# Score products of a gated recurrence on four groups of partitions, and two gate products moved between the last two heads

## The chip, the core and the metric

The kernel runs on one core of a Trainium2 chip. The metric is the time on the device of one execution, in microseconds (us). The core has a matrix engine (TensorE, PE in the profile; its loads of the stationary operand are listed apart as PEld), a vector engine (VectorE, DVE), a scalar engine (ScalarE, ACT), a general engine (GpSimd, POOL) and an engine that starts transfers (SyncE, SP). Each works through its own list in order, and they wait for each other by semaphores.

## The reference

Two layers on 1024 tokens of width 1024. Layer 0 is windowed attention; the change does not touch it. Layer 1 is a gated linear recurrence (HGRN2) with 8 heads of key and value width 128:

```python
proj = h @ w_in                       # q, f, i, z
q = silu(q)
log_f = logaddexp(log(lb), log1p(-lb) + log_sigmoid(f))
k = -expm1(log_f);  v = i
# per head, over time:  S = S * exp(log_f) + k v^T ;  o = q S
# in chunks: scores[t, s] = sum_k q[t] k[s] exp(b[t] - b[s])  for s <= t,  b = cumsum(log_f)
o = o * rsqrt(mean(o * o) + eps) * gnorm_w
y = (o * silu(z)) @ w_out
```

Each layer is wrapped in two norms and added to its input.

## The kernel before

All large projections are done in three products: both operands are split into a high and a low part, and `product` (L189) adds high x high, high x low and low x high. A projection of 128 x 512 is one unit of 24 such products, into one of two buffers of PSUM (tag "mm").

`mixer1` is layer 1. Its `plan` is a list of units in the order in which they are written: `i_unit` (values), `qf_unit` (q, and f with k, of one head in halves of 512 tokens), `rec(h)` (the recurrence of a head), `z_unit(c, t)` (the gate: a projection, a sigmoid on ScalarE at L868, a product on VectorE at L869, and one on GpSimd that multiplies it into the values, L870). The order of the plan gives priorities; the order on each engine is worked out by a scheduler from them, so that units of the plan interleave on the engines. What `rec(h)` needs on VectorE and GpSimd is done while TensorE works on the projections of the next unit.

`rec(h)` calls `scores_block` on the usual path (the other, `scores_tree`, is not run with these inputs). The tokens are in 8 blocks of 128, and keys stand in the stationary operand, queries in the moving one; the key width of 128 is summed over:

- Two scans on VectorE (L757, L758) give the running products U and V of the gate in sub-blocks of 16. Q and K are multiplied by them (L759, L760), and the totals of sub-blocks go to a small tile `tt` (L769 to L774). U and V are then reused for the scaled operands of the lowest level (L776 to L779); Q and K are scaled for the levels above (L780, L781), and from there are called X and Y.
- L788 computes all scores within blocks of 32 (32 products of 32 keys by 32 queries, tile `psd`). Output partition is key, and the 32 keys of a product lie at partitions 0, 32, 64 or 96: four groups in turns. L792 copies the causal part to the score tile `sc`.
- L797 computes the scores between the two blocks of 32 in a block of 64: 16 products of 32 by 32, into partitions 0 to 31 and 64 to 95 of `pss`. L801 copies them to `sc`.
- X and Y are scaled once more (L806 VectorE, L807 GpSimd), and L812 computes the scores between the two blocks of 64 in a block of 128: 8 products of 64 keys by 64 queries, all into partitions 0 to 63. L814 copies them.
- A last scaling gives the operands between blocks of 128. `rec` then transposes Y (L828), forms key-value products (L834), runs the state through the 8 blocks on VectorE (L838, L840), and adds scores x values (L847) and X x state (L849). Each half is normed (L852, L215, L217, L855).

The tiles `psd`, `pss` share two buffers of PSUM (tag "s"). Weights come in order through SP's queue, are split by ScalarE (L154) and VectorE (L155), and a weight's place is free for the next after its last product.

Of the kernel before, what the change touches and what calls it, by code (L numbers as in the profile page):

```python
# [12 lines left out]
F32 = mybir.dt.float32  # L13
# [4 lines left out]
AF = mybir.ActivationFunctionType  # L18
# [5 lines left out]
P = 128  # L24
# [65 lines left out]
def emit(tc, I, out):  # L90
    nc = tc.nc
# [3 lines left out]
    with top:  # L95
# [4 lines left out]
        pp = top.enter_context(tc.tile_pool(name="ps", bufs=2, space=PSUM))  # L100
# [565 lines left out]
        def mixer1(fast, vo, rp):  # L666
# [11 lines left out]
            def qf_unit(h, isf, half):  # L678
                ps = proj_feat(60 + 4 * h + 2 * isf + 8 * (h // 4), half)
                cs = slice(half * 512, (half + 1) * 512)  # L680
                if (h, isf) not in qfk:
                    if isf and fast:
                        qfk[h, 1] = Fs[h % 2]
                    else:
                        qfk[h, isf] = rp.tile([P, T], F32, tag="qf"[isf], bufs=2 if isf else nb3, name="qf")
                dst = qfk[h, isf][:, cs]
                if not isf:
                    sg = rp.tile([P, 512], F32, tag="sg", bufs=2, name="sg")
                    nc.scalar.activation(sg, ps, AF.Sigmoid)
                    v.tensor_tensor(dst, ps, sg, op=ALU.mult)  # L690
                else:
                    if (h, 2) not in qfk:
                        qfk[h, 2] = rp.tile([P, T], F32, tag="k", bufs=nb3, name="kk")
                    kk = qfk[h, 2][:, cs]
                    lb, ol = lbt[:, 1, h:h + 1], lbt[:, 0, h:h + 1]
                    nc.scalar.activation(dst, ps, AF.Sigmoid)  # L696
                    nc.scalar.activation(kk, ps, AF.Sigmoid, scale=-1.0)
                    nc.gpsimd.tensor_scalar(dst, dst, ol, lb, op0=ALU.mult, op1=ALU.add)  # L698
                    nc.gpsimd.tensor_scalar(kk, kk, ol, 1.0, op0=ALU.mult, op1=ALU.mult)
# [48 lines left out]
            def scores_block(h, Q, F, K):  # L748


                sc = scs[h % 2]

                v.tensor_copy(F1[:, ::16], F[:, :T:16])
                nc.gpsimd.memset(F[:, :T:16], 0.0)
                U = rp.tile([P, T], F32, tag="U", name="U")
                V = rp.tile([P, T], F32, tag="V", name="V")
                v.tensor_tensor_scan(U, F[:, :T], F1, 0.0, op0=ALU.mult, op1=ALU.add)  # L757
                v.tensor_tensor_scan(V[:, ::-1], F[:, T:0:-1], E1[:, ::-1], 0.0, op0=ALU.mult, op1=ALU.add)  # L758
                v.tensor_tensor(Q, Q, U, op=ALU.mult)  # L759
                v.tensor_tensor(K, K, V, op=ALU.mult)  # L760

                def blk(a, n):
                    return a.rearrange("p (b two n) -> p b two n", two=2, n=n)

                tt = rp.tile([P, 6, 32], F32, tag="tt", bufs=2, name="tt")
                t32, t64, t128 = tt[:, 4, :], tt[:, 5, :16], tt[:, 5, 16:24]
                e1, e2, r1, r2 = (tt[:, i, :].unsqueeze(2).to_broadcast([P, 32, 16]) for i in range(4))
                for i in range(2):
                    v.tensor_copy(tt[:, i, :], U[:, 16 * i + 15::32])  # L769
                v.reciprocal(tt[:, 2:4, :], tt[:, 0:2, :])  # L770
                v.tensor_tensor(t32, tt[:, 0, :], tt[:, 1, :], op=ALU.mult)
                for a, b in ((t64, t32), (t128, t64)):
                    bv = b.rearrange("p (b two) -> p b two", two=2)
                    v.tensor_tensor(a, bv[:, :, 0], bv[:, :, 1], op=ALU.mult)  # L774
                Q2, K2, M2, N2 = blk(Q, 16), blk(K, 16), blk(U, 16), blk(V, 16)
                v.tensor_tensor(M2[:, :, 0, :], Q2[:, :, 0, :], r1, op=ALU.mult)  # L776
                nc.gpsimd.tensor_copy(M2[:, :, 1, :], Q2[:, :, 1, :])
                nc.gpsimd.tensor_copy(N2[:, :, 0, :], K2[:, :, 0, :])
                v.tensor_tensor(N2[:, :, 1, :], K2[:, :, 1, :], r2, op=ALU.mult)  # L779
                v.tensor_tensor(Q2[:, :, 1, :], Q2[:, :, 1, :], e1, op=ALU.mult)  # L780
                nc.gpsimd.tensor_tensor(K2[:, :, 0, :], K2[:, :, 0, :], e2, op=ALU.mult)  # L781
                X, Y = Q, K

                ps = pp.tile([P, 8, 32], F32, tag="s", name="psd")
                for c in range(8):
                    for o in range(0, P, 32):
                        cs = slice(c * P + o, c * P + o + 32)
                        nc.tensor.matmul(ps[o:o + 32, c, :], V[:, cs], U[:, cs], start=True, stop=True)  # L788
                for o in range(0, P, 32):
                    r = slice(o, o + 32)  # L790
                    mk = msk[r, M_D - M_L + o:M_D - M_L + o + 32]
                    v.copy_predicated(sc[r, :, r], mk.unsqueeze(1).to_broadcast([32, 8, 32]), ps[r])  # L792
                ps = pp.tile([P, 8, 64], F32, tag="s", name="pss")
                for c in range(8):
                    for j in range(2):
                        o = c * P + 64 * j
                        nc.tensor.matmul(ps[64 * j:64 * j + 32, c, :32], Y[:, o:o + 32], X[:, o + 32:o + 64],  # L797
                                         start=True, stop=True)
                for j in range(2):
                    o = 64 * j  # L800
                    nc.scalar.activation(sc[o:o + 32, :, o + 32:o + 64], ps[o:o + 32, :, :32], AF.Copy)  # L801
                for n, tot in ((32, t32), (64, t64)):
                    Xv, Yv = blk(X, n), blk(Y, n)
                    nb = T // (2 * n)
                    tv = tot.rearrange("p (b two) -> p b two", two=2)
                    v.tensor_tensor(Xv[:, :, 1, :], Xv[:, :, 1, :], tv[:, :, 0:1].to_broadcast([P, nb, n]), op=ALU.mult)  # L806
                    nc.gpsimd.tensor_tensor(Yv[:, :, 0, :], Yv[:, :, 0, :], tv[:, :, 1:2].to_broadcast([P, nb, n]),  # L807
                                            op=ALU.mult)
                    if n == 32:
                        ps = pp.tile([P, 8, 64], F32, tag="s", name="pss")  # L810
                        for c in range(8):
                            nc.tensor.matmul(ps[:64, c, :], Y[:, c * P:c * P + 64], X[:, c * P + 64:(c + 1) * P],  # L812
                                             start=True, stop=True)
                        nc.scalar.activation(sc[:64, :, 64:], ps[:64], AF.Copy)  # L814
                return sc, X, Y, t128

            def rec(h):
                vt = vo[h // 4]
                hc = slice((h % 4) * P, (h % 4 + 1) * P)
                ins = (qfk[h, 0], qfk[h, 1], qfk[h, 2])  # L820
                sc, X, Y, tot = scores_block(h, *ins) if fast else scores_tree(*ins)
                yn = rp.tile([P, 8, P], F32, tag="yn", name="yn")
                S = rp.tile([P, 8, P], F32, tag="S", name="S")
# [41 lines left out]
            def z_unit(c, t):  # L865
                ps = proj_nat(100 + 8 * c, t)
                sg = rp.tile([P, 512], F32, tag="sg", bufs=2, name="sg")
                nc.scalar.activation(sg, ps, AF.Sigmoid)  # L868
                v.tensor_tensor(sg, ps, sg, op=ALU.mult)  # L869
                nc.gpsimd.tensor_tensor(vo[c][:, t, :], vo[c][:, t, :], sg, op=ALU.mult)  # L870

            QF = [(0, 0), (1, 0), (0, 1), (1, 1)]
            qf = lambda h: [lambda u=u: qf_unit(h, *u) for u in QF]
            iu = lambda c: [lambda t=t: i_unit(c, t) for t in range(8)]
            zu = lambda c: [lambda t=t: z_unit(c, t) for t in range(8)]
            rc = lambda h: [lambda: rec(h)]
            plan = iu(0) + qf(0) + ([zeros] if fast else []) + qf(1) + rc(0) + qf(2) + rc(1) + qf(3) + rc(2) + iu(1) + rc(3)
            plan += qf(4) + qf(5) + rc(4) + qf(6) + rc(5) + qf(7) + rc(6) + rc(7) + zu(0)
            for u in plan:
                u()  # L880
            for t in range(5):
# [163 lines left out]
```

## Time and profile before

| | |
|---|---|
| median of 3 runs | 920.67 us (918.2, 920.67, 920.74) |
| profiled execution | 919.34 us, span 917.5 us |
| granted TensorE clock | 0.995 of full, mean |
| TensorE busy | 891.1 us, 97% |
| VectorE / ScalarE / GpSimd busy | 551.2 / 373.7 / 342.1 us |
| the stage of the heads | about 480 to 745 us of the span |

The span runs from the first instruction to the last; what is left of the time lies around it. In the rows of the profile, a line such as L812 is a line of the kernel before; `out<-in` are the program's tile names; `128*32 128x32` is the shape of the array used and that of the operand. PE rows give matrix products, PEld rows loads of the stationary operand. A row of the timeline merges successive instructions of one line. In brackets stands the idle time ahead of the row and who ended it. The row of a stage gives start and end, its length, then busy time and count for PE, PEld, DVE, ACT and POOL, the granted clock, the share of the DMA engines and GB/s.

### The profile page before, as it was taken

How to read it: one execution, taken by the hardware profiler on the slowest of the kernel's cores; microseconds unless marked ns; L12 is line 12 of the kernel's file. 1: busy time of each engine (PE TensorE's matmuls, PEld its weight loads, DVE VectorE, ACT ScalarE, POOL GpSimd, SP SyncE). 2: the span in 40 equal slices, each digit the busy share in tenths (PEclk: the TensorE clock that was granted, in tenths of full speed). 3: DMA queues.
4: the chain of work that ended last, by engine and by line, in shares of the span. 5: the costliest groups of instructions: out<-in, count | busy, mean ns of one | idle time of the engine just before them, and what ended most of it. 6: DMA issues, size and time to landing. Idle time of an engine off the chain costs nothing.

```text
span 917.5 us, 14082 instructions
## 1 busy us (share of the span) xinstructions
PE 891.1 (97%) x5214; PEld 744.8 (81%) x5214; DVE 551.2 (60%) x911; ACT 373.7 (41%) x958; POOL 342.1 (37%) x506
## 2 busy tenths in 40 slices
PE   6989999999999999999999999999999999999996
PEld 4868888888887788878888888888888788888885
DVE  6858887777876535762278864246866924252243
ACT  6525667666656332542322331423334124242311
POOL 5504465667787202330054422115424433210011
PEclk9999999999999999999999999999999999999998
DMA  8455364512311223540311010121111003032053
GB/s 285 143 153 157 107 185 130 166 54 62 90 54 59 91 63 129 177 149 19 106 50 36 24 47 1 51 66 35 35 47 48 1 1 92 1 98 86 24 183 119
DMA packets 53255, 78.61 MB, mean 86 GB/s; under 512 B 4760, under 2 KB 24984, under 8 KB 53176
## 3 DMA queue, kind: packets, MB, share of 16 engines
q1 hardware_dynamic: 53032, 77.51, 27.5%
q8 instruction: 43, 0.70, 0.3%
q14 instruction: 36, 0.29, 0.1%
q10 hardware_dynamic: 144, 0.10, 0.1%
HBM read 58.89 MB, written 16.88 MB: 83 GB/s over the span
## 4 chain that ended last, share of the span: by engine, by line
PE 72%; POOL 9%; DVE 7%; issue 5%; DMA 3%; ACT 2%; SPq 0%; POOLq 0%; ACTq 0%; DVEq 0%
PE psmm L189 59%; POOL rstd L217 2%; PE psk L834 1%; PE pso L847 1%; PE pss L514 1%; PE pss L515 1%; POOL ms L215 1%; PE pso L849 1%; PE pst L535 1%; POOL mY L546 1%; POOL mY L549 1%; DMA sinT<-csd 1%; PE pss L812 1%; PE pst L828 1%; PE pst L861 1%
## 5 line engine op out<-in xcount | busy, mean ns | idle before, releaser
L189 PE MATMUL psmm<-acth,whi 128*128 128x512 f32 x528 | 210.0, 398 | 1.6 <-DVE th L474 1.1
L189 PE MATMUL psmm<-acth,wlo 128*128 128x512 f32 x528 | 208.1, 394 | 0.2 <-POOL wlo L155 0.2
L189 PE MATMUL psmm<-actl,whi 128*128 128x512 f32 x528 | 208.2, 394 | 0.0
L189 PE MATMUL psmm<-whi,acth 128*128 128x512 f32 (+1 forms) x520 | 202.4, 391 | 1.0 <-DVE y L616 0.6
L189 PE MATMUL psmm<-wlo,acth 128*128 128x512 f32 (+1 forms) x520 | 201.2, 388 | 0.0
L189 PE MATMUL psmm<-whi,actl 128*128 128x512 f32 (+1 forms) x520 | 201.2, 388 | 0.0
L155 DVE TENSOR_TENSOR wlo<-wraw,whi 128x512 fp32r<-128x512 f32 x126 | 93.5, 754 | 95.6 <-ACT whi L154 91.2
L189 PEld LDWEIGHTS psmm<-acth,whi 128*128 128x128 f32 x528 | 99.6, 189 | 21.9 <-DVE th L474 2.2
L189 PEld LDWEIGHTS psmm<-acth,wlo 128*128 128x128 f32 x528 | 99.5, 189 | 19.9 <-POOL wlo L155 0.6
L189 PEld LDWEIGHTS psmm<-whi,acth 128*128 128x128 f32 x520 | 97.7, 188 | 21.2 <-DVE th L474 0.9
L189 PEld LDWEIGHTS psmm<-actl,whi 128*128 128x128 f32 x528 | 99.7, 189 | 18.4
L189 PEld LDWEIGHTS psmm<-whi,actl 128*128 128x128 f32 x520 | 97.7, 188 | 20.3 <-DVE actl L593 0.8
L189 PEld LDWEIGHTS psmm<-wlo,acth 128*128 128x128 f32 x520 | 97.8, 188 | 19.1
L154 ACT ACTIVATE whi<-wraw 128x512 fp32r<-128x512 f32 x112 | 69.9, 630 | 85.5 <-PE psmm L189 66.4
L529 ACT ACTIVATE sm<-sm,st 128x129 f32<-128x129 f32 x128 | 50.0, 392 | 52.0 <-DVE st L527 52.0
L698 POOL TENSOR_SCALAR gate<-gate,lbt 128x512 f32<-128x512 f32 x16 | 17.7, 1108 | 121.8 <-ACT gate L696 121.8
L908 DVE TENSOR_TENSOR y<-psmm,wpost 128x512 f32<-128x512 f32 (+1 forms) x17 | 11.2, 660 | 53.7 <-ACT jk L907 50.7
L217 POOL TENSOR_TENSOR rstd<-ms,nhalf 128x1 f32<-128x1 f32 (+1 forms) x48 | 41.8, 870 | 3.8
L546 POOL TENSOR_SCALAR_AFFINE_SELECT mY<-pT 64x256 fp32r<-64x256 f32 x56 | 29.3, 523 | 31.8 <-ACT pT L538 26.8
L907 ACT ACTIVATE jk<-psmm 128x512 f32<-128x512 f32 (+1 forms) x17 | 9.7, 571 | 66.9 <-PE psmm L189 66.9
L514 PE MATMUL pss<-KH,QS 128*128 128x256 f32 (+1 forms) x128 | 32.9, 284 | 3.8 <-DMA QS<-qd 3.8
L549 POOL TENSOR_SCALAR_AFFINE_SELECT mY<-pT 64x256 fp32r<-64x256 f32 x64 | 30.8, 481 | 6.0 <-ACT pT L538 1.4
(225 smaller groups left out, 1432.0 us busy)
## 6 DMA issues: line engine op xcount, KB each, us to landing
wraw<-in_w SPq DMA_DIRECT2D x132, 256.0 KB
QS<-qd SPq DMA_DIRECT2D x16, 512.0 KB
xr<-in_x SPq DMA_DIRECT2D x8, 512.0 KB
x1d<-xn SPq DMA_DIRECT2D x8, 512.0 KB
xr<-x1d SPq DMA_DIRECT2D x8, 512.0 KB
out_dram<-xn SPq DMA_DIRECT2D x16, 256.0 KB
xh<-in_x SPq DMA_DIRECT2D x4, 512.0 KB
qd<-qh SPq DMA_DIRECT2D x8, 256.0 KB
```

The source lines that it names most:

```text
L154: nc.scalar.activation(hi, raw, AF.Copy)
L155: W["split_ins"][i] = (nc.gpsimd if on_pool else v).tensor_tensor(lo, raw, hi.bitcast(F32), op=ALU.subtract)
L189: nc.tensor.matmul(ps, a, b, start=(k == 0 and i == 0), stop=(k == NK - 1 and i == 2))
L215: keep(nc.gpsimd.tensor_scalar(m, ms, eps, 1.0, op0=ALU.add, op1=ALU.mult))
L217: W["rstd"] = keep(nc.gpsimd.tensor_tensor(r, m, nhalf[:, :width], op=ALU.pow))
L514: nc.tensor.matmul(ps[:, i, :nkk], q, KH[:, g, k0:k0 + nkk], start=True, stop=False)
L529: nc.scalar.activation(sm[:, h, :], sm[:, h, :], AF.Exp, bias=nm[:, h:h + 1], scale=0.125, accum_out=dn[:, h:h + 1])
L546: nc.gpsimd.affine_select(mY[r, :, :64], src[64:, :, :64].bitcast(F32), [[0, 4], [-1, 64]], ALU.is_gt, 0.0, base=0, channel_multiplier=1)
L549: nc.gpsimd.affine_select(mY[r, :, 64:], src[:64, :, 64:].bitcast(F32), [[0, 4], [1, 64]], ALU.is_ge, 0.0, base=0, channel_multiplier=-1)
L698: nc.gpsimd.tensor_scalar(dst, dst, ol, lb, op0=ALU.mult, op1=ALU.add)
L907: nc.scalar.activation(jk[:, c0:c1], ps, AF.Square, scale=D ** -0.5, accum_out=ss)
L908: v.tensor_tensor(y[:, c0:c1], ps, wpost[:, c * 512 + c0:c * 512 + c1], op=ALU.mult)
```

## The change

In `scores_block`, L797's 16 products are the same, but they go to four groups of partitions in place of two: block of 64 number j and block of 128 number c take partitions 64j + 32(c mod 2) on. The 64-key products of L812 are cut into two of 32 keys by 64 queries, whose outputs go to partitions 0, 32, 64 and 96 in turns. Because even and odd blocks now lie in different partitions, the copies to `sc` are cut too: four of 32 partitions x 128 columns in place of two of 32 x 256, and two of 64 x 256 in place of one of 64 x 512. The two tiles are half as wide. In the plan, the first two `z_unit`s of column half 0 stand ahead of `rec(7)`.

```diff
-                ps = pp.tile([P, 8, 64], F32, tag="s", name="pss")
+
+                ps = pp.tile([P, 4, 32], F32, tag="s", name="pss")
                 for c in range(8):
                     for j in range(2):
-                        o = c * P + 64 * j
-                        nc.tensor.matmul(ps[64 * j:64 * j + 32, c, :32], Y[:, o:o + 32], X[:, o + 32:o + 64],
-                                         start=True, stop=True)
-                for j in range(2):
-                    o = 64 * j
-                    nc.scalar.activation(sc[o:o + 32, :, o + 32:o + 64], ps[o:o + 32, :, :32], AF.Copy)
+                        o, q = c * P + 64 * j, 64 * j + 32 * (c % 2)
+                        nc.tensor.matmul(ps[q:q + 32, c // 2, :], Y[:, o:o + 32], X[:, o + 32:o + 64], start=True, stop=True)
+                for o in (0, 64):
+                    for q in range(2):
+                        nc.scalar.activation(sc[o:o + 32, q::2, o + 32:o + 64], ps[o + 32 * q:o + 32 * q + 32], AF.Copy)
...
                     if n == 32:
-                        ps = pp.tile([P, 8, 64], F32, tag="s", name="pss")
+                        ps = pp.tile([P, 4, 64], F32, tag="s", name="psq")
                         for c in range(8):
-                            nc.tensor.matmul(ps[:64, c, :], Y[:, c * P:c * P + 64], X[:, c * P + 64:(c + 1) * P],
-                                             start=True, stop=True)
-                        nc.scalar.activation(sc[:64, :, 64:], ps[:64], AF.Copy)
+                            for o in (0, 32):
+                                q = 64 * (c % 2) + o
+                                nc.tensor.matmul(ps[q:q + 32, c // 2, :], Y[:, c * P + o:c * P + o + 32],
+                                                 X[:, c * P + 64:(c + 1) * P], start=True, stop=True)
+                        for q in range(2):
+                            nc.scalar.activation(sc[:64, q::2, 64:], ps[64 * q:64 * q + 64], AF.Copy)
...
-            plan += qf(4) + qf(5) + rc(4) + qf(6) + rc(5) + qf(7) + rc(6) + rc(7) + zu(0)
+            plan += qf(4) + qf(5) + rc(4) + qf(6) + rc(5) + qf(7) + rc(6) + zu(0)[:2] + rc(7) + zu(0)[2:]
```

Below L797 the line numbers shift: L797 becomes L798, L812 becomes L814, L814 becomes L817, and what follows in `rec` moves by 3.

The order on TensorE in head 0, at the upper level; `qf` and `kk` are X and Y, and `psmm` is a projection of the next head:

```order
 L189 MATMUL psmm<-actl_0_105,whi_80 128x512
 L189 MATMUL psmm<-acth_0_104,wlo_90 128x512
-L812 MATMUL pss<-qf,kk 64x64 x8
+L814 MATMUL psq<-qf,kk 32x64 x16
 L189 MATMUL psmm<-acth_0_108,whi_80 128x512
 L189 MATMUL psmm<-actl_0_109,whi_80 128x512
```

The sixteen smaller products stand where the eight stood.

The order on TensorE between heads 6 and 7: `psd` is head 7's lowest level, `pst` the transposes of head 6, `psmm` a gate product of `z_unit`:

```order
 L189 MATMUL psmm<-whi_84,acth_0_120 128x512
 L189 MATMUL psmm<-wlo_94,acth_0_120 128x512
+L189 MATMUL psmm<-whi_84,actl_0_121 128x512
 L788 MATMUL psd<-U,V 32x32 x7
-L828 MATMUL pst<-cst,kk 128x128 x8
+L831 MATMUL pst<-cst,kk 128x128 x8
 L788 MATMUL psd<-U,V 32x32 x25
```

One product of the gate has moved ahead of head 7's first scores, from behind its second ones; 62 others of the `z_unit`s stood between head 6's and head 7's first scores already. From head 7's chain on, the list of TensorE is otherwise as it was; in heads 0 to 5, places of whole rows move by one to eight products of L189.

The order on ScalarE in head 0, at the copies of the scores:

```order
 L697 ACTIVATE kk<-psmm 128x512
-L801 ACTIVATE sc_4165<-pss 32x8x32 x2
-L689 ACTIVATE sg<-psmm 128x512
-L814 ACTIVATE sc_4165<-pss 64x8x64
+L801 ACTIVATE sc_4165<-pss 32x4x32 x4
+L689 ACTIVATE sg<-psmm 128x512
+L817 ACTIVATE sc_4165<-psq 64x4x64 x2
 L696 ACTIVATE gate_4169<-psmm 128x512
```

Six copies stand where three stood, with the same neighbours. SP's list of transfers is unchanged.

## Prediction

> **What bounds the kernel now.** First the engine table and the chain of waits on the page, then the busy time of the stage that the change touches (480 to 745 us, the eight heads), then the waits of TensorE in that stretch. An arrow names who was waited for; behind the colon stand us in total, times, and the longest.
>
> ```profile
> PE 891.1 (97%) x5214; PEld 744.8 (81%) x5214; DVE 551.2 (60%) x911; ACT 373.7 (41%) x958; POOL 342.1 (37%) x506
> PE 72%; POOL 9%; DVE 7%; issue 5%; DMA 3%; ACT 2%; SPq 0%; POOLq 0%; ACTq 0%; DVEq 0%
> 480.00:745.00 265.00, 263.88 (x2134) 221.99 (x2134) 169.53 (x258) 85.41 (x233) 92.69 (x101) 1.00 0.12 35
> PE psd L788 <- DVE tt L774: 0.9, 1, 0.9
> PE psmm L189 <- DVE qf L690: 0.2, 1, 0.2
> ```
>
> TensorE (PE) is busy 263.88 of the stage's 265.00 us at the full granted clock (1.00), ScalarE (ACT) 85.41, VectorE (DVE) 169.53. TensorE waits only twice, 1.1 us together. So whatever shortens TensorE's own stream here shortens the run, until an order of work on VectorE takes over; the two waits show where that is nearest.
>
> **The score products.** The timeline of TensorE around head 0 (start, length, engine, line, shape, count; a run of like instructions is merged). Each product of float32 operands shows as two passes, so L788's 32 products are 64, L797's 16 are 32 and L812's 8 are 16.
>
> ```profile
> 479.74 0.39 PE L189 MATMUL psmm<-acth,wlo 128*128 128x512 f32 x1
> 480.06 0.79 PE L788 MATMUL psd<-U,V 128*32 128x32 f32 x64
> 480.70 0.70 PE L797 MATMUL pss<-qf,kk 128*32 128x32 f32 x32
> 481.33 0.50 PE L189 MATMUL psmm<-acth,whi 128*128 128x512 f32 x1
> ...
> 487.15 0.39 PE L189 MATMUL psmm<-actl,whi 128*128 128x512 f32 x1
> 487.38 0.39 PE L189 MATMUL psmm<-acth,wlo 128*128 128x512 f32 x1
> 487.69 1.15 PE L812 MATMUL pss<-qf,kk 128*64 128x64 f32 x16
> 488.77 0.50 PE L189 MATMUL psmm<-acth,whi 128*128 128x512 f32 x1
> ```
>
> And the durations of single instructions by line (min/median/max ns), loads of the stationary operand (PEld) and products:
>
> ```profile
> L788 PEld LDWEIGHTS psd<-U,V x512: 106/111/113, 480.1 to 727.7; 128*32 128x32 f32 x171
> L788 PE MATMUL psd<-U,V x512: 189/196/217, 480.1 to 727.8; 128*32 128x32 f32 x171
> L797 PE MATMUL pss<-qf,kk x256: 189/196/217, 480.7 to 730.5; 128*32 128x32 f32 x128
> L812 PEld LDWEIGHTS pss<-qf,kk x128: 132/138/138, 487.7 to 740.5; 128*64 128x64 f32 x128
> L812 PE MATMUL pss<-qf,kk x128: 222/222/270, 487.7 to 740.6; 128*64 128x64 f32 x128
> ```
>
> A run is its steps plus the last pass, so the mean step from start to start is (length minus one median pass) over (count minus one): L788 (0.79 − 0.196)/63 = 9.4 ns on four groups in turns; L797 (0.70 − 0.196)/31 = 16.3 ns on two; L812 (1.15 − 0.222)/15 = 61.9 ns on one. The reader is to see that step times groups is nearly the same for the two 32-key lines (38 and 33 ns): a group takes about 33 ns for a pass, and the groups work at the same time.
>
> *32-key level (L797, now L798).* Same 32 passes, on four groups in place of two. Step: between half of 16.3 (8.1) and L788's 9.4, so the run is 31 x 8.1 to 9.4 + 0.196 = 0.45 to 0.49 us against 0.70. I take 0.23 us saved per head.
>
> *64-key level (L812, now L814).* Eight products of 64 keys by 64 queries become sixteen of 32 keys by 64 queries: twice the passes, four groups in place of one. Such a pass (loads 32 wide, streams 64) stands in no row, so it is bounded. If the stream alone sets its time in a group, it stays at 61.9 ns; if load and stream count alike, it lies halfway between 33 and 61.9, at 47. From 32 to 64 wide on both sides the step of one group rises by 29 ns, the load's duration by 27 (111 to 138) and the product's by 26 (196 to 222): one of them, not their sum, so load and stream overlap, and the 64 columns that still stream set the time. I take 61.9: step 61.9/4 = 15.5, run 31 x 15.5 + 0.222 = 0.70 us, 0.45 saved; the other end, 47/4 = 11.8, gives 0.59 us, 0.56 saved. The bound on the bad side is no overlap at all with 64 columns streaming: 31 x 61.9 + 0.222 = 2.14 us, 0.99 lost.
>
> The Trainium skill, "TensorE: Matmul & The Clock Gate", section "Wait — 56ns, not 53.3ns?", says that products never start closer than about 25 ns, however short. By it L798 would gain nothing and L814 would take about 31 x 25 + 222 = 997 ns, an estimate from that page, and little of the gain would remain; the trace disagrees, with L788 at 9.4 ns.
>
> Per head 0.23 + 0.45 = 0.68 us, over eight heads 5.4. The changes between array shapes (128*128 to narrower and back) stay as many as before, so their cost falls out.
>
> **The evictions.** ScalarE's copies of these scores, from the groups of that stretch and around head 6:
>
> ```profile
> L801 ACT ACTIVATE sc<-pss 32x256 f32<-32x256 f32 x16 | 5.9, 368 | 2.9 <-PE pss L797 2.7
> 719.72 0.59 ACT L814 ACTIVATE sc<-pss 64x512 f32<-64x512 f32 x1 [3.88 <-PE pss L812]
> 736.23 0.49 PE L847 MATMUL pso<-vo,sc 128*128 128x128 f32 x3
> ```
>
> Two of 32x256 and one of 64x512 become four of 128 columns and two of 256. From 256 to 512 columns a copy rises from 368 to 590 ns, 0.87 ns per column, so 128 columns cost about 257: 4 x 257 + 2 x 368 = 1764 ns against 2 x 368 + 590 = 1326, 0.44 us more per head. I cost it at nothing: the scores are wanted by L847, 15.9 us after the last copy ended here (720.31 to 736.23), and ScalarE is idle two thirds of the stage. Were that cover gone, it would be 3.5 us over eight heads.
>
> **The gate products between heads 6 and 7.** The listing of TensorE's order moves one product of 128x512 from behind head 7's scores to ahead of them; the other products of the two units stood there already. No DMA moves on SP's queue. That place, on TensorE and VectorE:
>
> ```profile
> 724.73 0.39 PE L189 MATMUL psmm<-wlo,acth 128*128 128x512 f32 x1
> 726.04 0.33 PE L788 MATMUL psd<-U,V 128*32 128x32 f32 x14 [0.92 <-DVE tt L774]
> ```
> ```profile
> 709.03 0.43 DVE L792 COPY_PREDICATED sc<-msk,psd 32x256 f32<-32x256 uint8 x1 [1.87 <-PE psd L788]
> 709.77 0.69 DVE L855 TENSOR_TENSOR vo<-pso,rstd 128x512 f32<-128x512 f32 x1 [0.30 <-POOL rstd L217]
> 710.47 1.39 DVE L792 COPY_PREDICATED sc<-msk,psd 32x256 f32<-32x256 uint8 x3
> ...
> 724.35 1.54 DVE L779 TENSOR_TENSOR V<-kk,tt 128x512 f32<-128x512 f32 x1
> 725.81 0.16 DVE L774 TENSOR_TENSOR tt<-tt 128x16 f32<-128x16 f32 x1
> ```
>
> Head 7's L788 needs V. VectorE begins when head 6's L788 is done (709.03) and works without a gap from 709.77 to 725.97, while TensorE, with less to do, waits 0.92 us. Between these two L788 lie head 6's two shortened runs. That stretch is VectorE's, so its 0.68 us only lengthens the wait: late next is TensorE, by 0.92 + 0.68 − 0.23 = 1.37 us, where 0.23 is the product pulled in (487.38 − 487.15). Nothing is queued behind the wait that another engine needs sooner than head 7. Kept of head 6: 0.23 in place of 0.68.
>
> **Sum.** 5.4 − 0.68 + 0.23 = 5.0 us off. The profiled execution took 919.34 us, so 914.3 on its own scale; it lies 0.4 us below the mean of all four executions (920.74, 918.2, 920.67 and itself: 919.74), so I put the median at **914.7 us**. The median shown, 920.67, is the top of that scatter.
>
> **Rivals.** *VectorE takes over in more heads.* TensorE reuses a buffer of projections only when VectorE has emptied it, and in a head that copy sits in VectorE's queue. The first pair is head 1's preparation, the second head 6's:
>
> ```profile
> 492.09 0.69 DVE L690 TENSOR_TENSOR qf<-psmm,sg 128x512 f32<-128x512 f32 x1
> ...
> 689.70 0.68 DVE L690 TENSOR_TENSOR qf<-psmm,sg 128x512 f32<-128x512 f32 x1
> ```
> ```profile
> 493.66 0.39 PE L189 MATMUL psmm<-acth,whi 128*128 128x512 f32 x1
> ...
> 691.06 0.39 PE L189 MATMUL psmm<-acth,whi 128*128 128x512 f32 x1
> ```
>
> The buffer is free 0.88 us (492.78 to 493.66) and 0.68 us (690.38 to 691.06) before it is used, and both shortened runs lie between head start and that use. 0.68 saved just fits; if VectorE runs half a us later in four such heads, they keep 0.2 each, and the gain falls to 5.0 − 4 x 0.5 = 3.0, time 916.7. For it: the margins are this thin. Against: in head 6's preparation the new order puts that copy ahead of a reciprocal (0.5 us), so the margin grows there.
>
> *Starts limited.* The new runs start passes no faster than L797 does now, 16.3 ns: L798 saves nothing, L814 31 x 16.3 + 0.222 = 0.73, 0.42 saved; 8 x 0.42 − 0.42 + 0.23 = 3.2, time 916.5. Against it stands L788's 9.4. The floor of 25 ns that the Trainium skill's page "TensorE: Matmul & The Clock Gate" gives would, put into the same sum as an estimate, leave about 1.3 us of gain and 918.4.
>
> *Slower: pieces with 64 streamed columns do not overlap.* Step 61.9 for twice the passes: 0.99 lost less 0.23 in each head, 8 x 0.76 = 6.1 us, time 925.8. It decides from a step of (1.15 + 0.23 − 0.222)/31 = 37 ns on. Against it: L788 overlaps its four groups fully with 32 columns.
>
> *The copies are not hidden*: 3.5 us come back, time 918.2. *The plan does nothing*: the move of two units is nearly that already, and is costed so.
>
> **How the numbers follow.** Chances: forecast 66%, VectorE in more heads 17%, limited starts 6%, copies exposed 5%, slower rival 6%. About 0.3%, 2.8 us, can be told from no change, so faster means under 917.9. The forecast (66), the limited starts (6) and half of the first rival (8) lie there: faster 0.80. Its other half (9), where VectorE takes more than I worked out, and the copies (5) make the same 0.14; the slower rival is 0.06. The range's low end takes 0.25 + 0.56 per head: 8 x 0.81 − 0.81 + 0.23 = 5.9, 913.8, and 1.5 for the scatter of the runs shown: 912.2. The high end, 917.4, takes in the first two rivals at 916.7 with half of that scatter.
>
> **What would show it.** L798's run of 32 passes near 0.47 us and L814's of 32 near 0.70; 1.4 us of wait ahead of head 7's L788; L690 no longer ahead of its buffer's reuse by more than a few tenths; TensorE's busy time in this stage down by about 5 to 5.5 us and ScalarE's up by 3.5. Wrong would be: L814 over 1.0 us, waits of TensorE on VectorE in other heads over 1 us together, or TensorE waiting on ScalarE's copies.

## The result, and the profile after

| | before | after |
|---|---|---|
| median of 9 runs each | 919.86 us (918.2 to 921.32) | 915.41 us (913.67 to 916.93) |
| ratio, 95% interval | | 0.995 (0.9939 to 0.9961) |
| profiled execution: time, span | 919.34, 917.5 us | 915.41, 913.7 us |

4.45 us faster; 5.0 had been forecast, from the mean of four earlier executions. The kernel gained in the stage of the heads, and where it did not gain, VectorE set the pace.

The page of the changed kernel, engine table; then its timeline of TensorE around head 0, and the durations of the two new lines:

```profile
PE 886.2 (97%) x5342; PEld 738.1 (81%) x5342; DVE 553.8 (61%) x911; ACT 377.6 (41%) x982; POOL 341.2 (37%) x506
```
```profile
480.83 0.87 PE L788 MATMUL psd<-U,V 128*32 128x32 f32 x64
481.55 0.46 PE L798 MATMUL pss<-qf,kk 128*32 128x32 f32 x32
...
488.28 0.65 PE L814 MATMUL psq<-qf,kk 128*32 128x64 f32 x32
```
```profile
L798 PE MATMUL pss<-qf,kk x256: 189/196/218, 481.5 to 727.4; 128*32 128x32 f32 x128
L814 PEld LDWEIGHTS psq<-qf,kk x256: 106/110/111, 488.3 to 736.9; 128*32 128x32 f32 x128
L814 PE MATMUL psq<-qf,kk x256: 218/219/244, 488.3 to 736.9; 128*32 128x64 f32 x128
```

L798's run of 32 passes takes 0.46 us in place of 0.70, L814's 0.65 in place of 1.15. The mean steps are (0.46 − 0.196)/31 = 8.5 ns and (0.65 − 0.219)/31 = 13.9 ns. TensorE is busy 4.9 us less, ScalarE 3.9 us more.

The same place between heads 6 and 7, on TensorE and on VectorE:

```profile
701.58 0.38 PE L788 MATMUL psd<-U,V 128*32 128x32 f32 x20
...
723.08 0.33 PE L788 MATMUL psd<-U,V 128*32 128x32 f32 x14 [1.35 <-DVE tt L774]
```
```profile
706.80 0.69 DVE L858 TENSOR_TENSOR vo<-pso,rstd 128x512 f32<-128x512 f32 x1 [0.23 <-POOL rstd L217]
707.51 1.38 DVE L792 COPY_PREDICATED sc<-msk,psd 32x256 f32<-32x256 uint8 x3
...
721.39 1.54 DVE L779 TENSOR_TENSOR V<-kk,tt 128x512 f32<-128x512 f32 x1
722.86 0.16 DVE L774 TENSOR_TENSOR tt<-tt 128x16 f32<-128x16 f32 x1
```

TensorE now waits 1.35 us there (0.92 before), and the stretch from head 6's L788 to head 7's is as long as it was: before, head 6's began at

```profile
704.54 0.38 PE L788 MATMUL psd<-U,V 128*32 128x32 f32 x20
```

and head 7's at 726.04, which is 21.50 us; now 723.08 − 701.58 = 21.50. The starts of L788 cut both executions into stretches:

| from head's L788 to the next | 0 | 1 | 2 | 3 | 4 | 5 | 6 | 7 to the end |
|---|---|---|---|---|---|---|---|---|
| before, us | 27.09 | 30.72 | 55.93 | 41.44 | 38.57 | 30.73 | 21.50 | 191.49 |
| after, us | 26.43 | 30.26 | 55.18 | 40.77 | 37.85 | 30.26 | 21.50 | 190.60 |
| gained | 0.66 | 0.46 | 0.75 | 0.67 | 0.72 | 0.47 | 0.00 | 0.89 |

Together 4.6 us. What lies ahead of head 0 was not touched and differs from execution to execution (head 0 began between 478.7 and 482.7 us in the profiles of this study), so the stretch from head 0 to the end is the better measure for comparing single profiles: 437.5 us before, 432.9 after.

### The profile page after: what moved, and what is told of

It reads as the page before. It is cut to its first block, busy times and chain, and to the rows that moved or that the text cites. A ratio compares the mean times of both kernels' runs of the same rounds, so it can differ in the third digit from the quotient of the medians.

```text
span 913.7 us, 14363 instructions
## 1 busy us (share of the span) xinstructions
PE 886.2 (97%) x5342; PEld 738.1 (81%) x5342; DVE 553.8 (61%) x911; ACT 377.6 (41%) x982; POOL 341.2 (37%) x506
## 4 chain that ended last, share of the span: by engine, by line
PE 72%; POOL 9%; DVE 8%; issue 5%; DMA 3%; ACT 2%; SPq 0%; POOLq 0%; ACTq 0%; DVEq 0%
PE psmm L189 60%; POOL rstd L217 2%; PE psk L837 1%; PE pso L850 1%; PE pss L515 1%; PE pss L514 1%; POOL ms L215 1%; PE pso L852 1%; PE pst L535 1%; POOL mY L546 1%; POOL mY L549 1%; DMA sinT<-csd 1%; PE pst L831 1%; PE pst L864 1%; ACT sm L529 1%
## 5 line engine op out<-in xcount | busy, mean ns | idle before, releaser
L189 PE MATMUL psmm<-acth,whi 128*128 128x512 f32 x528 | 209.9, 398 | 1.8 <-DVE th L474 1.0
L189 PE MATMUL psmm<-acth,wlo 128*128 128x512 f32 x528 | 208.5, 395 | 0.2 <-POOL wlo L155 0.2
L189 PE MATMUL psmm<-actl,whi 128*128 128x512 f32 x528 | 208.2, 394 | 0.0
L189 PE MATMUL psmm<-whi,acth 128*128 128x512 f32 (+1 forms) x520 | 202.8, 391 | 1.0 <-DVE y L616 0.6
L189 PE MATMUL psmm<-whi,actl 128*128 128x512 f32 (+1 forms) x520 | 201.3, 388 | 0.0
L189 PE MATMUL psmm<-wlo,acth 128*128 128x512 f32 (+1 forms) x520 | 200.9, 387 | 0.0
L189 PEld LDWEIGHTS psmm<-acth,whi 128*128 128x128 f32 x528 | 99.6, 189 | 22.8 <-DVE th L474 2.1
L189 PEld LDWEIGHTS psmm<-acth,wlo 128*128 128x128 f32 x528 | 99.6, 189 | 20.0 <-POOL wlo L155 0.6
L189 PEld LDWEIGHTS psmm<-whi,acth 128*128 128x128 f32 x520 | 97.7, 188 | 21.4 <-DVE y L616 0.9
L189 PEld LDWEIGHTS psmm<-actl,whi 128*128 128x128 f32 x528 | 99.7, 189 | 18.2
L189 PEld LDWEIGHTS psmm<-whi,actl 128*128 128x128 f32 x520 | 97.7, 188 | 20.1 <-DVE actl L593 0.6
L189 PEld LDWEIGHTS psmm<-wlo,acth 128*128 128x128 f32 x520 | 97.8, 188 | 19.1
L546 POOL TENSOR_SCALAR_AFFINE_SELECT mY<-pT 64x256 fp32r<-64x256 f32 x56 | 29.3, 523 | 31.5 <-ACT pT L538 26.4
L179 ACT ACTIVATE acth<-pst,cst 128x512 fp32r<-128x512 f32 x48 | 29.6, 692 | 8.4 <-PE pst L237 8.4
```

The costliest lines, as they stand in the source:

```text
L179: ins = nc.scalar.activation(hi, ps, AF.Copy, scale=scale)
L189: nc.tensor.matmul(ps, a, b, start=(k == 0 and i == 0), stop=(k == NK - 1 and i == 2))
L546: nc.gpsimd.affine_select(mY[r, :, :64], src[64:, :, :64].bitcast(F32), [[0, 4], [-1, 64]], ALU.is_gt, 0.0, base=0, channel_multiplier=1)
```

## The experiments

The theory: the groups of partitions work at the same time, a group's pass is set by the longer of its load and its stream, and what that saves counts wherever TensorE is not waiting for VectorE, which by the prediction is so everywhere but in head 6. The rivals: the smaller pieces themselves pay; VectorE caps every head; the moved gate products make the difference.

**One level at a time.** Each has one of the two blocks of the change and otherwise the kernel before; in the first the 64-key block stays as it was, in the second the 32-key block. Against the change, the first:

```diff
-                            for o in (0, 32):
-                                q = 64 * (c % 2) + o
-                                nc.tensor.matmul(ps[q:q + 32, c // 2, :], Y[:, c * P + o:c * P + o + 32],
-                                                 X[:, c * P + 64:(c + 1) * P], start=True, stop=True)
+                            nc.tensor.matmul(ps[:64, c, :], Y[:, c * P:c * P + 64], X[:, c * P + 64:(c + 1) * P],
+                                             start=True, stop=True)
```

and the second:

```diff
-                        o, q = c * P + 64 * j, 64 * j + 32 * (c % 2)
-                        nc.tensor.matmul(ps[q:q + 32, c // 2, :], Y[:, o:o + 32], X[:, o + 32:o + 64], start=True, stop=True)
+                        o = c * P + 64 * j
+                        nc.tensor.matmul(ps[64 * j:64 * j + 32, c, :32], Y[:, o:o + 32], X[:, o + 32:o + 64],
+                                         start=True, stop=True)
```

The copies and tiles go with them, and the plan is that of before.

> Only the 32-key level on four groups; the 64-key level and the plan as before. Theory (TensorE's own time, capped by VectorE in head 6): 32 passes at 8.5 in place of 16.2 ns, 0.24 us in each of seven heads and the one moved product for head 6: about 1.9 us off, 918.0 against 919.9; the wait ahead of head 7's L788 grows from 0.9 to about 0.9. Rival (VectorE's order caps every head, so either part alone would give nearly the whole): 3 us or more off.

Measured: 917.83 us, ratio 0.9984 (0.9972 to 0.9996); the wait ahead of head 7 is 0.9 us; from head 0 to the end 435.6 us, 1.9 below before.

> Only the 64-key level cut to pieces of 32 keys on four groups. Theory: L814's run 0.65 in place of 1.15 us, 0.49 us in seven heads and 0.23 for the moved product: about 3.6 us off, 916.2; wait ahead of head 7's L788 about 1.15. With the 32-key part alone it adds up to the whole change's 4.5 within 1 us (5.5). Rival (VectorE caps every head): 4.4 off alone, as much as the whole.

Measured: 916.52 us, ratio 0.9961 (0.9946 to 0.9975); wait 1.2 us; from head 0 to the end 433.9, 3.6 below. The answers of the waits, first of the one, then of the other:

```profile
PE psd L788 <- DVE tt L774: 0.9, 1, 0.9
```
```profile
PE psd L788 <- DVE tt L774: 1.2, 1, 1.2
```

Beside 919.90 for the kernel before on the same chip, that is 2.1 and 3.4 us less. By the stretches the parts add up to 1.9 + 3.6 = 5.5 us, 0.9 more than the whole change gains. Head 6 is no part of this: its stretch is 21.50 us in both runs, as before and after. Of the 0.9, 0.44 lies behind head 7's start, where each of the two runs has the one gate product that moved (0.23 us) and the change has it once, too; 0.21 lies in head 5 and 0.12 in head 1. Head 5 gained 0.23 us by the one part and 0.45 by the other (30.50 and 30.28 us against 30.73), but 0.47 by both; this is taken up below. That VectorE caps every head is out: then either part alone would have had nearly the whole gain, 3 us or more, and the interval of the first ends at 2.6.

**The plan.** The edit of the plan is taken back, the rest of the change stays (only the end of the plan's line is printed):

```diff
-rc(6) + zu(0)[:2] + rc(7) + zu(0)[2:]
+rc(6) + rc(7) + zu(0)
```

> The change without its edit of the plan. Theory: that edit alters nothing, since the lists of all engines come out the same with and without it: the time of the change, 915.4, with a wait of 1.35 us ahead of head 7's L788. Rival (the moved units are what brings the one product ahead): 0.2 us slower, wait 1.6.

Measured: 915.34 us, ratio 0.9958 (0.9942 to 0.9974), from head 0 to the end 433.1 us, wait 1.3 us. The edit of the plan does nothing: the lists of all five engines are the same with and without it, on the kernel before as well. The one product stands ahead of head 7's L788 also in the two runs with one level alone, whose plan is that of before. What is left is that the scheduler, given other score products, ordered anew.

**More gate products.** Three units in place of two (the end of the plan's line again):

```diff
-zu(0)[:2] + rc(7) + zu(0)[2:]
+zu(0)[:3] + rc(7) + zu(0)[3:]
```

> The change with three units of the gate ahead of the last head in place of two. Nine more products (2.0 us) then stand ahead of head 7's L788. Theory (TensorE waits there for VectorE alone): the wait of 1.35 us goes, time 1.3 us below the change, 914.1. Rival (head 7's chain, begun 0.7 us later, is then late at its own end): a new wait behind it, no gain.

Measured: 913.94 us, ratio 0.9939 (0.9925 to 0.9954); from head 0 to the end 431.4 us, 1.46 below the change. The timeline of TensorE ahead of head 7, where L788 now follows six of head 6's transposes without idle time:

```profile
721.70 0.82 PE L831 MATMUL pst<-cst,kk 128*128 128x128 f32 x6
722.45 0.68 PE L788 MATMUL psd<-U,V 128*32 128x32 f32 x54
```

The wait is gone, and no new one stands behind it: the stretch from head 6 to 7 grew from 21.50 to 22.99 us for 2.04 us of gate products and 0.75 us of transposes moved into it in place of the wait, and what follows fell from 190.6 to 187.7. On the same chip its median is 1.4 us below that of the run before it, which is the change in all but name (915.34).

**What pays, pieces or groups.** The 64-key level as eight whole products of 64 keys by 64 queries, even and odd blocks on two groups:

```diff
-                            for o in (0, 32):
-                                q = 64 * (c % 2) + o
-                                nc.tensor.matmul(ps[q:q + 32, c // 2, :], Y[:, c * P + o:c * P + o + 32],
...
+                            q = 64 * (c % 2)
+                            nc.tensor.matmul(ps[q:q + 64, c // 2, :], Y[:, c * P:c * P + 64],
...
```

> The change, but the 64-key level in whole products of 64 keys by 64 queries on two groups in turns (even and odd blocks), 16 passes. Theory (groups work at the same time; the stream sets a group's pass): step 61.6/2 = 31 ns, run 15 x 31 + 222 = 0.69 us against 0.65: within 0.3 us of the change, 915.6. Rival (the smaller pieces themselves are what pays): run near 1.15, 4 us slower than the change, 919.

Measured: 914.81 us, ratio 0.994 (0.9921 to 0.996); from head 0 to the end 432.5 us. Its run:

```profile
490.11 0.69 PE L813 MATMUL psq<-qf,kk 128*64 128x64 f32 x16
```

0.69 us with half as many passes: (0.69 − 0.222)/15 = 31 ns, half of the 61.9 of one group. Cutting the pieces added nothing that two groups had not given. What counts is the number of passes times the length of a group's pass, divided by the number of groups in turns.

**What sets a group's pass.** The same work in pieces of 64 keys by 32 queries on two groups, so that load and stream change places:

```diff
-                        for c in range(8):
-                            for o in (0, 32):
-                                q = 64 * (c % 2) + o
-                                nc.tensor.matmul(ps[q:q + 32, c // 2, :], Y[:, c * P + o:c * P + o + 32],
-                                                 X[:, c * P + 64:(c + 1) * P], start=True, stop=True)
+                        for c2 in range(4):
+                            for o in (0, 32):
+                                for e in range(2):
+                                    c, q = 2 * c2 + e, 64 * e
+                                    nc.tensor.matmul(ps[q:q + 64, c2, o:o + 32], Y[:, c * P:c * P + 64],
+                                                     X[:, c * P + 64 + o:c * P + 96 + o], start=True, stop=True)
```

> The change, but the 64-key level in pieces of 64 keys by 32 queries on two groups in turns, 32 passes: the load is 64 wide, the stream 32. It tells what sets a group's pass. If load and stream overlap and the longer sets it: 61.6/2 = 31 ns, run 1.15 us, 8 x 0.5 less the 0.5 that head 6's wait gives back: 3.5 us slower than the change, 919. If the stream alone sets it: 16.2 ns, run 0.70 us, 915.8. If load and stream add up: 47/2 = 23 ns, run 0.93, 917.3.

Measured: 920.23 us, ratio 1.0002 (0.9989 to 1.0014). Its run in head 0, and the durations:

```profile
488.54 1.13 PE L815 MATMUL psq<-qf,kk 128*64 128x32 f32 x32
```
```profile
L815 PEld LDWEIGHTS psq<-qf,kk x256: 132/138/138, 488.5 to 740.9; 128*64 128x64 f32 x128
L815 PE MATMUL psq<-qf,kk x256: 222/223/244, 488.5 to 740.9; 128*64 128x32 f32 x128
```

(1.13 − 0.223)/31 = 29 ns on two groups, 58 ns for a pass: with a load of 64 and a stream of 32 a group's pass is as long as with a load of 32 and a stream of 64 (56 ns), while 32 and 32 take 33. For these pieces the longer of the two sets it; that the stream alone does (a step of 16 ns) or that they add up (23) is out, and the change itself rules out the load alone. The load is as wide as the part of the array that is used, and no run here separates the two.

The time is 1.2 us above what was expected. The scheduler cut this run in two in five heads, 13 runs for 8 heads. A cut costs about 0.32 us: 0.32 us pass from the last wide product to the first pass, 0.15 from the last pass to the next wide product and 0.34 to the one after it, where wide products stand 0.23 apart, less the one step that it replaces. Against it, head 4's L788 is in one piece there, and not in two. Two gate products also moved back behind head 7's L788, where the wait is 1.0 us. What each has of the 1.2 us was not told apart.

**Turns.** The sixteen pieces of the change in another order, the four of one group one after the other:

```diff
-                        for c in range(8):
-                            for o in (0, 32):
-                                q = 64 * (c % 2) + o
+                        for q in range(0, P, 32):
+                            for c in range(q // 64, 8, 2):
+                                o = q % 64
```

> The change, but the sixteen pieces of the 64-key level group by group, four on one group in a row, in place of turns. Theory (a group's pass takes 56 ns, and TensorE takes products in order): three in four passes wait for their own group: 31 x 56 less the overlap at three changes of group, about 1.8 us a run: 8 x 1.15 less 1.35 that head 6's wait absorbs: 8 us slower than the change, 923. Rival (TensorE reorders by group, so turns don't matter): 0.65 us, 915.4.

Measured: 920.52 us, ratio 1.0013 (0.9997 to 1.0028). Its run, and the wait ahead of head 7:

```profile
488.13 1.39 PE L814 MATMUL psq<-qf,kk 128*32 128x64 f32 x32
```
```profile
PE psd L788 <- DVE tt L774: 0.6, 1, 0.6
```

Without turns the run takes 1.39 us, longer than the eight whole products did on one group (1.15): 8 x 0.74 less the 0.75 that the wait gives back is 5.2 us. The medians of this run and of the change (915.41) differ by 5.1, their profiles from head 0 to the end by 4.4 (437.3 and 432.9). So turns decide. The size was missed: 1.8 us had been expected from passes that wait for their own group, with a mean step of 50 ns, but it is 38. In the single records the first passes, all of one group, follow at 56 ns, but at the first change of group two start within 6 ns, and from there most come two in 56 ns, so TensorE works on part of the next group's passes beside them.

**Both together, and the change again.** `e8_two64_z3` joins three gate units with the whole products on two groups; `e9_change_again` is the change.

> Three units of the gate ahead of the last head, and the 64-key level as eight whole products on two groups in turns. Theory: the two add nothing to each other; the time of the run with three units alone, 913.9, within 0.5, and no wait ahead of head 7's L788. Rival (head 7's lowest level moves ahead of the chain's end again, as the order on TensorE is different from that run): a wait of 0.5 us or more, 914.5.

Measured: 914.36 us, ratio 0.9946 (0.9928 to 0.9963), no wait ahead of head 7, from head 0 to the end 431.9 us. That is within half a us of three units alone, as expected, and no better. Beside the whole products on two groups without the third unit (432.5 us, and a wait of 0.9), filling the wait is worth 0.6 us here, and the median is 0.4 below that of the change on the same chip, less than the noise.

> The change itself once more beside it. Theory: 915.4, wait of 1.35 us ahead of head 7's L788, TensorE's first product after the emptied buffer late by 0.2 to 0.3 us in head 5. Rival (those lateness figures are accidents of one execution): they change by more than 0.2 us.

Measured: 914.73 us, ratio 0.9944 (0.9928 to 0.996); wait 1.4 us; from head 0 to the end 432.7 us (432.9 and 433.1 in the change's other two profiles). The lateness in head 5, shown below, is there again, 0.17 us.

## Why the prediction was right

*TensorE bounds the stage.* Right: 4.9 us less of its busy time, 4.45 us less in all.

*The 32-key level*, 0.23 us per head: measured 0.24 (step 8.5 ns, between the bounds 8.1 and 9.4). The rival of limited starts, 16.3 ns, is out.

*The 64-key level*, 0.45 us: measured 0.50. The choice that the stream sets a group's pass and overlaps the load was right, though a little high: the step is 13.9 and not 15.5 ns, 56 ns for a group's pass in place of 61.9. Part of this is the reading of the row: of L812's single records the first step is 107 ns and all others are 58 or 59, so the mean of 61.9 puts what the run's start costs once on every pass. The slower rival, which needed a step over 37 ns, is out. The exchange of load and stream shows the reason behind the choice: the longer of the two sets it.

*The Trainium skill's floor* of about 25 ns between starts ("TensorE: Matmul & The Clock Gate", section "Wait — 56ns, not 53.3ns?") does not hold across groups here: 8.5, 9.4 and 13.9 ns.

*The evictions*, costed at nothing: right. ScalarE is busy 3.9 us more (3.5 forecast), and no wait of TensorE on those copies appeared.

*Head 6 given to VectorE*: right to a few hundredths, a wait of 1.35 us against 1.37, and the stretch unchanged at 21.50 us. That VectorE alone held it is shown by the run with three units, where the wait was filled with products, and by the runs with one level alone: the wait was 0.9 and 1.2 us, the stretch 21.50 in both.

*The gate products*: the size (one product, 0.23 us) was right, the cause wrong. It was put down to the edit of the plan; that edit does nothing.

*The first rival, VectorE in more heads*, has come true in one head. The forecast of 0.68 us per head would "just fit" the margins; with 0.74 it no longer does in head 5. The rows of the copy and of TensorE's products there, in the changed kernel:

```profile
687.21 0.68 DVE L690 TENSOR_TENSOR qf<-psmm,sg 128x512 f32<-128x512 f32 x1
```
```profile
687.66 0.39 PE L189 MATMUL psmm<-acth,wlo 128*128 128x512 f32 x1
687.95 0.50 PE L189 MATMUL psmm<-acth,whi 128*128 128x512 f32 x1
688.28 0.39 PE L189 MATMUL psmm<-actl,whi 128*128 128x512 f32 x1
```

The buffer is free at 687.89, the product starts at 687.95, and it and the next come 0.29 and 0.33 us after the one ahead of them, where 0.23 is the rule: 0.17 us lost. Against it the prediction had said that the new order moves this copy ahead of a reciprocal there; it stood ahead of it already (689.70 and 690.30 before), so that comfort was misread. In the two runs with one level alone no product comes late there: head 5's margin holds either part and not both, as the 0.23, 0.45 and 0.47 us above show. Heads 1 and 5 gained 0.46 and 0.47 us where the others, head 6 apart, gained 0.66 or more. In head 1, L788 took 0.08 us longer (below), its first product that reuses the buffer came 0.03 late, and L798's first pass came 0.16 us after L788's last, in place of 0.04. With three units this gap is 0.04 again, but a product comes 0.11 late and the head is no shorter (30.24 us), so what holds head 1 stays open.

*The sum*: by the measured sizes 8 x 0.74 − 0.74 + 0.23 = 5.4 us, 4.6 seen from head 0 to the end. Of the 0.8 between, 0.3 is L788, which became longer in the heads outside head 6, 0.17 the late products in head 5 and 0.15 the gap and the late product in head 1; the rest was not told apart. That the forecast of 5.0 came so near is in part luck: the levels gained 0.4 us more over seven heads than forecast, and this hid half of the losses, of which the sum had none.

## What to carry to other kernels

The float32 products of 32 and 64 columns here gained from being spread over groups of partitions in turns: the step between passes was that of one group (33 ns with 32 columns loaded and streamed, 56 to 62 where either was 64) divided by the number of groups, so try to spread such products over groups before cutting them into pieces. Once TensorE is shortened, look for the stretch that another engine holds, since there the gain only becomes a wait, and fill it with work that is ready; here that was worth 1.4 us in one version and 0.6 in another. And look at the order that the scheduler made before believing that an edit of a plan moved anything.

## What had not been expected

L788 itself is unchanged, but takes longer in the changed kernel: its mean step, over all heads, is 10.1 ns and was 9.5, 0.34 us in all; in head 0 its run takes 0.87 us in place of 0.79. In head 0 the steps of its first 32 passes are as before (32 ns for four); those of the second half are uneven in both kernels, and longer in the changed one. It is so in every kernel whose 64-key level has 32 passes (10.0 to 10.2) and in none with 16 (9.4 to 9.5). The cause was not tested and stays open.
